# Two-layer hybrid decoder trunk: the first layer's loads in one written order, scale vectors turned on TensorE, bias table behind the projections

## The chip, the core and the metric

One core of a Trainium2 chip runs the whole program. Its engines work side by side, each through its own instruction stream in a fixed order: TensorE (PE) for products and transposes, VectorE (DVE), ScalarE (ACT), GpSimd (POOL), and SyncE (SP), which here issues the DMAs. An instruction that waits holds up all that stand behind it on its engine. The metric is device time in microseconds: the profiled execution took 2197.31 us, and the three timed runs 2196.4 to 2206.05 us.

## The reference

Two layers over 1024 tokens of width 1024, all in fp32. Each layer normalises, makes one projection of 1312 columns and gives its parts to three mixers; their outputs are concatenated, projected and added; then comes a SwiGLU feed-forward part.

```python
for l in range(DEPTH):
    h = rms_norm(x, attn_norm[l])
    proj = h @ w_in[l]                                   # 1024 x 1312
    q_a, k_a, v_a, u_b, cq_c, ckv_c, kr_c = jnp.split(proj, split_idx, axis=-1)
    out_a = swa_mixer(q_a, k_a, v_a, swa_q_gain[l], swa_k_gain[l], swa_sinks[l], rel_bias)
    out_b = pool_mixer(u_b, pool_w[l], pool_scale[l])
    out_c = mla_mixer(cq_c, ckv_c, kr_c, positions, ...)
    x = x + jnp.concatenate([out_a, out_b, out_c], axis=-1) @ w_out[l]
    h = rms_norm(x, ffn_norm[l])
    x = x + (jax.nn.silu(h @ w_gate[l]) * (h @ w_up[l])) @ w_down[l]
```

The sliding-window mixer (`swa_mixer`) adds a relative-position bias of 128 x 256 per head, made from a 32-row table; the latent-attention mixer (`mla_mixer`) turns parts of its queries and keys by the cosine and sine of position times frequency. Gains are vectors that scale columns.

## The kernel before, in words

The kernel is written with a planner: the program gives instructions and their dependences, the planner runs a simulation of the engines and writes each engine's order. Two means bend that order: a block of high priority, and `issue_after(i)`, which puts instructions behind `i` on their engine's queue without waiting for more than that. Tiles come from pools; a pool with `bufs=n` has n buffers for a name, and a load into one waits until the readers of its old content are done.

Each layer has `phase1` (projection, sliding-window and pooling mixers), `phase2` (latent attention and output projection) and `phase34` (feed-forward). All products of fp32 values are made of three passes, high part with high, high with low, low with high; so every weight is split into two tiles: ACT scales and rounds it to the high part (L351), DVE subtracts to get the low part (L352).

`phase1` works on eight tiles of 128 tokens, t = 0 to 7. `head(t)` (L330) squares the rows of x for the norm and turns the tile on PE in eight transposes, splitting it into `hT`. The weights of `w_in` (1024 x 1312) come in three column blocks of 512, 400 and 400, each in eight row blocks of 128 (L345 to L352): a load by SP into `raw` (five buffers), scaled by the norm's gain `gn`, a vector loaded element by element with rows on partitions (L316). `wa` holds the first block, `wb` the other two. For each tile `proj(0, 512)` (24 products, L381 to L383) gives q and k, which become `qk` (L390), are normalised, turned by transposes `tq` and scaled by `gq` into `qs`; `proj(512, 512)` and `proj(1024, 288)` give the rest. The accumulators `acc` have two banks, so the first group of tile 1 comes behind the last of tile 0. Then come the transposes of the pooling and latent parts, the scores `s` of the sliding window, the bias added (L523), the exponentials (L528), transposes `tp` of the weights and the product with `vt` (L543, L544).

`tables` (L133), called once in layer 0 behind the weight loop, builds what all tiles need. The bias: a small product of `rel` and `hot` (L146), copied into `flip` (L148), written to DRAM as `rows` (L150), read back with overlapping rows into `T`, which borrows the key tile `kr5` (L153), reversed by a product with `flip` (L159), copied to `bias` (L160) and kept in DRAM for layer 1 (L161). The gains: `gq`, `gk`, `pscale`, `gc`, `gm`, `gmk` are loaded element by element into columns (L175 to L204). The angles: some 45 short DVE instructions on tiles `rr` that borrow five `raw` buffers, and two sines on ACT (L207 to L280). The remaining tiles of x (L172) are loaded here too, in a chain of `issue_after`. The weights of layer 0 stand in a high-priority block, `tables` does not.

`phase2` loads `mla_w_kvb` and `mla_w_qb` (L589, L596) and scales their splits by `gc`; `early_out` (L806) loads parts of `w_out` into `raw3`, splits them into `wo0` to `wo4`, and multiplies with `mh`, adding rows `xt` of the input. `gn2`, the gain of the feed-forward norm spread to all partitions, is loaded at L875; the planner may issue that as soon as its buffer is free. The pools of `phase2` are laid over those of `phase1` in memory, so its first loads and writes wait for particular tiles of `phase1`.

Of the kernel before, what the change touches and what calls it, by code (L numbers as in the profile page):

```python
# [36 lines left out]
def trunk(ctx: ExitStack, tc: tile.TileContext, A, out):  # L37
# [55 lines left out]

    with tc.high_priority():
        sy.dma_start(xrow[0], A["x"][0, 0:P, :])
        sy.dma_start(ident, A["ident"])
# [6 lines left out]
    for l in range(DEPTH):  # L103
        xsrc = A["x"][0] if l == 0 else xres
        G = dict(
            ident=ident, xm=xm, xrow=xrow, krr=krr, rc=rc, cosT=cosT, sinT=sinT, sinks=sinks,
            pscale=pscale, invc=invc, nhalf=nhalf, gq=gq, gm=gm, cmask=cmask, identr=identr, rn=rn, gc=gc, g32=g32, xsrc=xsrc, dram=dram, gap=gap, xp=xp, gns=ExitStack(), bias_keep=bias_keep)
        phase1(nc, tc, A, l, pool, split, f, bcast, G, (gq, gk, gmk, dram) if l == 0 else None)
# [24 lines left out]
def tables(nc, tc, load, A, bcast, early, one, evq, ps, kr5, G, more):  # L133
    ve, sc, gp, te, sy = nc.vector, nc.scalar, nc.gpsimd, nc.tensor, nc.sync
    gq, gk, gmk, dram = more
    gm, sinks, bias, cosT, sinT = G["gm"], G["sinks"], G["bias"], G["cosT"], G["sinT"]

    rel = one.tile([P, 6], F32, name="rel")
    gp.memset(rel, NEG)
    sy.dma_start(rel[0:32], A["rel_bias"])  # L140
    hot = evq.tile([P, 512], F32, name="hot", tag="qk")[:, 0:384]
    sy.dma_start(hot[0:33], A["hot"])
    flip = evq.tile([P, 5, 128], F32, name="flip", tag="dup")
    sy.dma_start(flip[:, 0], A["flip"])
    acc = ps.tile([P, 512], F32, name="po")
    te.matmul(acc[0:6, 0:384], rel[0:33], hot[0:33], start=True, stop=True)  # L146
    vec = flip[0:6, 1:4]
    sc.copy(vec, acc[0:6, 0:384].rearrange("p (a b) -> p a b", a=3))  # L148
    rows = dram.tile([6, 384], F32, name="rows")
    sy.dma_start(rows.rearrange("h (a b) -> h a b", a=3), vec)  # L150
    base = rows[0:6, 0:256]
    T = kr5.bitcast(F32).rearrange("p a b c -> p (a b c)")
    sy.dma_start(T.rearrange("p (h j) -> p h j", h=6),  # L153
                 bass.AP(base.tensor, base.offset, [[1, P], [384, 6], [1, 256]]))
    b2 = bias.rearrange("p h j -> p (h j)")
    for i in range(3):
        acc = ps.tile([P, 512], F32, name="po")
        c = slice(512 * i, 512 * i + 512)
        te.matmul(acc, flip[:, 0], T[:, c], start=True, stop=True)  # L159
        sc.copy(b2[:, c], acc)  # L160
    sy.dma_start(G["bias_keep"], bias)  # L161

    pin = [load]

    def after(*calls):
        with tc.issue_after(pin[0].ins):
            for call in calls:
                last = call()
        pin[0] = last

    def xload(t):
        return sy.dma_start(G["xrow"][t], A["x"][0, t * P : (t + 1) * P, :])  # L172

    for h in range(2):
        after(lambda: sy.dma_start(gq[64 * h : 64 * h + 64], A["swa_q_gain"].rearrange("l d -> d l")),  # L175
              lambda: sy.dma_start(gk[64 * h : 64 * h + 64], A["swa_k_gain"].rearrange("l d -> d l")))
    ve.scalar_tensor_tensor(out=gq, in0=gq, scalar=0.125, in1=gk, op0=ALU.mult, op1=ALU.mult)
    after(lambda: xload(2))
    after(lambda: sy.dma_start(
        sinks, A["swa_sinks"].rearrange("l h -> (l h)").unsqueeze(0).to_broadcast([P, 12])  # L180
        .rearrange("p (l h) -> p l h", l=DEPTH)))
    after(lambda: sy.dma_start(G["invc"], A["invc"]))
    after(lambda: sy.dma_start(G["pscale"], A["pool_scale"].rearrange("l (k p) -> p l k", p=P)))
    slots = [early.tile([P, 4, NT, 16], F32, name="rr", tag="raw", bufs=5) for _ in range(5)]
    free = [t[:, i] for t in slots for i in range(4)]
    ps0 = free.pop().rearrange("p a b -> p (a b)")
    pos, posf, ifr = ps0[:, 0:8].bitcast(I32), ps0[:, 8:16], ps0[:, 16:32]
    after(lambda: sy.dma_start(pos, A["positions"][0].rearrange("(t p) -> p t", p=P)))
    ve.tensor_copy(posf, pos)
    after(lambda: sy.dma_start(ifr, bcast(A["invf"], 16)))  # L190
    for t in range(3, NT):
        after(lambda: xload(t))
    for l in range(DEPTH):
        after(lambda: sy.dma_start(G["gc"][:, l, 0:2], A["mla_q_a_gain"][l].rearrange("(k p) -> p k", p=P)))
        after(lambda: sy.dma_start(G["gc"][:, l, 2:3], A["mla_kv_a_gain"][l].rearrange("(k p) -> p k", p=P)))
        after(lambda: sy.dma_start(G["g32"][l], bcast(A["mla_q_rope_gain"][l], 32)))
    mask = one.tile([P, P], F32, name="mask", tag="ub")
    after(lambda: sy.dma_start(mask, A["cmask"]))
    sc.copy(G["cmask"], mask)
    sc.copy(G["identr"], G["ident"])  # L200
    gp.memset(gm, 1.0)
    gp.memset(gmk, 1.0)
    after(lambda: sy.dma_start(gm[0:64], A["mla_q_nope_gain"].rearrange("l d -> d l")))
    after(lambda: sy.dma_start(gmk[0:64], A["mla_k_nope_gain"].rearrange("l d -> d l")))  # L204
    ve.scalar_tensor_tensor(out=gm, in0=gm, scalar=float(96.0 ** -0.5), in1=gmk, op0=ALU.mult, op1=ALU.mult)
# [77 lines left out]
def phase1(nc, tc, A, l, pool, split, f, bcast, G, setup):  # L283
# [3 lines left out]
    with ExitStack() as ph:  # L287
# [26 lines left out]
        gn = early.tile([P, KT], F32, name="gn")  # L314
        with tc.high_priority() if l == 0 else nullcontext():
            sy.dma_start(gn, A["attn_norm"][l].rearrange("(k p) -> p k", p=P))  # L316
# [11 lines left out]
        behind = []  # L328

        def head(t):  # L330
# [3 lines left out]
            rows[t] = rstd_of(nc, ms, 1, G["nhalf"])  # L334
            hT = hTs[t] = hp[t % 2].tile([P, 2, KT, P], F32R, name="hT")
            for h in range(2):
# [3 lines left out]
                split(hT[:, 0, 4 * h : 4 * h + 4], hT[:, 1, 4 * h : 4 * h + 4], tp)  # L340

        with tc.high_priority() if l == 0 else nullcontext():
            if l == 0:
                head(0)
            for i, (c0, n) in enumerate(((0, 512), (512, 400), (912, 400))):  # L345
                for k in range(KT):
                    raw = early.tile([P, 512], F32, name="raw", bufs=5)[:, 0:n]
                    load = sy.dma_start(raw, A["w_in"][l, k * P : (k + 1) * P, c0 : c0 + n])
# [957 lines left out]
```

## Time and profile before

| | us |
|---|---|
| median of three runs | 2201.54 |
| lowest and highest run | 2196.4, 2206.05 |
| profiled execution | 2197.31 |
| its span, first to last instruction | 2195.5 |
| PE busy in it | 2104.7 |
| DVE, ACT, POOL busy | 1697.9, 1089.6, 974.3 |

In the profile's rows a timeline line gives the start in us, the duration in us, the engine, the source line, the operation, the tile written and those read, partitions by elements, and in brackets how long the engine had been idle and what it had waited for. SPq is the DMA issuer: its duration is that of the issue, not of the transfer. In a table by stretches each engine's busy time is followed by its count of instructions, then come the clock granted to PE (1.00 is full), the mean share of the DMA engines and GB/s.

### The profile page before, as it was taken

To read this page: it belongs to the slowest core of one execution; us is meant where nothing else is said; L and a number is where in the kernel's file an instruction comes from. 1 tells how busy PE (TensorE), PEld (TensorE's weight loads), DVE (VectorE), ACT (ScalarE), POOL (GpSimd) and SP (SyncE) were. 2 spreads that over 40 slices of the span, in tenths; PEclk is the share of its full clock that TensorE was granted. 3 is DMA by queue.
4 is the path that set the end of the run, shared out by engine and by line. 5 is a ranking of instruction groups with operands and counts; after the bars stand their busy time and mean duration, and the time that the engine had idled before them with its cause. 6 is when DMAs were issued, how large, how long until landed. Compare 5 with 4: busy or idle time off the path is not lost.

```text
span 2195.5 us, 29665 instructions
## 1 busy us (share of the span) xinstructions
PE 2104.7 (96%) x10420; PEld 1757.7 (80%) x10420; DVE 1697.9 (77%) x2595; ACT 1089.6 (50%) x2300; POOL 974.3 (44%) x916
## 2 busy tenths in 40 slices
PE   6998999999999999999989989999999999999999
PEld 4887788877888888788868867888778888887887
DVE  5567889889988888765765678887998888877657
ACT  5778667564344434321257786776634343343111
POOL 1433656336545443532613445462564544425215
PEclk8999999999999999999999999999999999999999
DMA  7002211234443434985540022113244443459754
GB/s 221 1 1 77 77 68 49 96 98 146 152 162 135 163 134 151 411 344 187 186 157 1 1 90 87 63 49 121 81 144 169 148 163 135 152 218 412 271 201 163
DMA packets 137933, 312.16 MB, mean 142 GB/s; under 512 B 17298, under 2 KB 68153, under 8 KB 137785
## 3 DMA queue, kind: packets, MB, share of 16 engines
q1 hardware_dynamic: 137784, 310.27, 39.7%
q8 instruction: 83, 1.36, 0.3%
q14 instruction: 66, 0.53, 0.1%
HBM read 203.53 MB, written 106.70 MB: 141 GB/s over the span
## 4 chain that ended last, share of the span: by engine, by line
PE 71%; DVE 11%; DMA 8%; ACT 5%; issue 2%; POOL 2%; SPq 1%; DVEq 0%; ACTq 0%; POOLq 0%
PE gu L1156 10%; PE gu L1154 10%; PE gu L1155 10%; PE dn L1001 5%; PE dn L1003 5%; PE dn L1002 5%; PE acc L381 3%; PE acc L382 3%; PE acc L383 3%; DMA rw<-in_w_down_dram 2%; PE tp L763 2%; PE po L804 1%; PE po L802 1%; DMA ga<-gd 1%; PE po L803 1%
## 5 line engine op out<-in xcount | busy, mean ns | idle before, releaser
L1156 PE MATMUL gu<-T,sb 128*128 128x512 f32 x704 | 275.2, 391 | 8.8 <-DVE sb L58 8.7
L1154 PE MATMUL gu<-T,sb 128*128 128x512 f32 x704 | 275.0, 391 | 3.9 <-DVE B L58 1.6
L1155 PE MATMUL gu<-T,sb 128*128 128x512 f32 x704 | 274.2, 390 | 0.0
L1001 PE MATMUL dn<-op,ga 128*128 128x512 f32 x616 | 240.1, 390 | 8.1 <-DMA ga<-gd 8.1
L1002 PE MATMUL dn<-op,ga 128*128 128x512 f32 x616 | 240.4, 390 | 0.0
L58 ACT CAST go<-xm 128x512 fp32r<-128x512 f32 x154 | 94.9, 620 | 292.3 <-POOL xm L1188 103.0
L1003 PE MATMUL dn<-op,ga 128*128 128x512 f32 x616 | 239.7, 390 | 0.0
L950 POOL TENSOR_TENSOR rw<-rw 128x1536 f32<-128x1536 f32 (+1 forms) x32 | 112.0, 3511 | 253.7 <-DVE op L960 160.6
L1131 POOL TENSOR_TENSOR xm<-raw 128x512 f32<-128x512 f32 x44 | 67.2, 1529 | 325.8 <-DMA raw<-in_w_up_dram 136.6
L959 ACT CAST op<-rw 128x1536 fp32r<-128x1536 f32 (+1 forms) x56 | 76.8, 1376 | 261.6 <-PE dn L1003 250.6
L58 DVE TENSOR_TENSOR go<-xm,go 128x512 fp32r<-128x512 f32 x154 | 157.5, 1033 | 41.1 <-ACT go L58 37.0
L58 ACT CAST sb<-raw 128x512 fp32r<-128x512 f32 x180 | 110.3, 616 | 115.3 <-PE gu L1156 92.2
L1156 PEld LDWEIGHTS gu<-T,sb 128*128 128x128 f32 x704 | 132.2, 188 | 40.1 <-DVE sb L58 12.9
L1154 PEld LDWEIGHTS gu<-T,sb 128*128 128x128 f32 x704 | 132.2, 188 | 33.7 <-ACT sb L58 3.5
L1188 POOL TENSOR_TENSOR xm<-xm 128x512 f32<-128x512 f32 x88 | 142.8, 1631 | 28.6 <-DVE go L58 18.4
L58 DVE TENSOR_TENSOR sb<-raw,sb 128x512 fp32r<-128x512 f32 x180 | 154.0, 856 | 0.9
L1155 PEld LDWEIGHTS gu<-T,sb 128*128 128x128 f32 x704 | 132.3, 188 | 27.7
L960 DVE TENSOR_TENSOR op<-rw,op 128x1536 fp32r<-128x1536 f32 (+1 forms) x56 | 113.8, 2032 | 40.7 <-ACT op L959 39.7
L1001 PEld LDWEIGHTS dn<-op,ga 128*128 128x128 f32 x616 | 116.0, 188 | 33.7 <-issue 8.6
L1154 PE MATMUL gu<-B,A 128*128 128x512 f32 x336 | 132.5, 395 | 3.9 <-ACT B L58 3.9
L1003 PEld LDWEIGHTS dn<-op,ga 128*128 128x128 f32 x616 | 116.0, 188 | 24.3
L1002 PEld LDWEIGHTS dn<-op,ga 128*128 128x128 f32 x616 | 115.9, 188 | 24.0
(324 smaller groups left out, 6084.3 us busy)
## 6 DMA issues: line engine op xcount, KB each, us to landing
gd<-go SPq DMA_DIRECT2D x154, 512.0 KB, 2.9
ga<-gd SPq DMA_DIRECT2D x154, 512.0 KB, 5.8
raw<-in_w_gate_dram SPq DMA_DIRECT2D x22, 1024.0 KB, 5.7
raw<-in_w_up_dram SPq DMA_DIRECT2D x22, 1024.0 KB, 6.6
rw<-in_w_down_dram SPq DMA_DIRECT2D x44, 512.0 KB, 8.0
xp<-xt SPq DMA_DIRECT2D x32, 256.0 KB, 2.0
old<-xp SPq DMA_DIRECT2D x16, 512.0 KB, 4.3
xp<-xm SPq DMA_DIRECT2D x16, 512.0 KB, 2.9
```

The costliest lines, as they stand in the source:

```text
L58: return sc.copy(hi, src), ve.tensor_tensor(out=lo, in0=src, in1=f(hi), op=ALU.subtract)
L950: gp.tensor_tensor(out=o, in0=a, in1=b, op=ALU.subtract)
L959: sc.copy(t[:, 0], q[b])
L960: ve.tensor_tensor(out=t[:, 1], in0=q[b], in1=f(t[:, 0]), op=ALU.subtract)
L1001: te.matmul(acc, S_[:, j, 0, ts], T_[:, 0, j], start=j == 0, stop=False)
L1002: te.matmul(acc, S_[:, j, 0, ts], T_[:, 1, j], start=False, stop=False)
L1003: te.matmul(acc, S_[:, j, 1, ts], T_[:, 0, j], start=False, stop=j == h - 1)
L1131: gp.tensor_tensor(out=s1, in0=q["A21"], in1=q["A22"], op=ALU.add)
L1154: te.matmul(acc, s[:, 0, k], b[:, 0, k], start=k == 0, stop=False)
L1155: te.matmul(acc, s[:, 0, k], b[:, 1, k], start=False, stop=False)
L1156: te.matmul(acc, s[:, 1, k], b[:, 0, k], start=False, stop=k == HK - 1)
L1188: gp.tensor_tensor(out=q[o], in0=q[a], in1=q[b], op=op)
```

## The change

Layer 0's start is rewritten as a class `Boot`; `tables` is dissolved into it.

- One order for the DMAs of the start: `load` puts each behind the one before on SP. Only four go by ACT's queue: the identity, the attention norm's gain of both layers, and the two gains of the sliding window.
- `raw` has eleven buffers in layer 0 instead of five; hot rows, the read-back table, angles and mask use them too.
- Vectors are loaded as rows (`gv`) and turned on PE (`turn`): `gna` (both layers' norm gains, at the start), `gqk` (behind tile 0's first group), `gains` (14 columns, behind tile 0's projections). Layer 1 copies its `gn` from `gna` on POOL.
- `head(0)` squares its rows only after its first split. Tile 1 is loaded and made ready between the first column block and the others; its first projection group (`group0(1)`) goes ahead of tile 0's second.
- A small load stands behind each weight of the second and third blocks (`steps`); the table is read back after the last weight (`fourth`), in three pieces; the bias products come behind tile 0's projections and pooling part (`bias`).
- In all tiles of both layers `proj(512, 512)` is queued behind the last product named in `G["mm"]`; `gn2` is queued behind the load of `mla_w_qb`.

```diff
+class Boot:
+    def load(self, dst, src):
+        if self.pin is None:
+            self.pin = self.nc.sync.dma_start(dst, src)
+        else:
+            with self.tc.issue_after(self.pin.ins):
+                self.pin = self.nc.sync.dma_start(dst, src)
+        return self.pin
+    def raw(self):
+        return self.early.tile([P, 512], F32, name="raw", bufs=11)
+    def turn(self, dst, rows, n):
+        te, sc = self.nc.tensor, self.nc.scalar
+        acc = self.psg.tile([P, 4, P], F32, name="ta")
+        te.transpose(acc[:, 0, 0:n], rows[0:n], self.G["ident"][0:n, 0:n])
+        sc.copy(dst, acc[:, 0, 0:n])
+    def first(self):
...
+        self.xload(0)
+        sc.dma_start(G["ident"], A["ident"])
+        sc.dma_start(gv[0:16, 0], A["attn_norm"].rearrange("l (k p) -> (l k) p", p=P))
+        for r, n in ((0, "swa_q_gain"), (2, "swa_k_gain")):
+            sc.dma_start(gv[r : r + 2, 2].rearrange("l (a d) -> l a d", a=2), A[n].unsqueeze(1).to_broadcast([2, 2, 64]))
+        self.nc.gpsimd.memset(gv[:, 1], 1.0)
+        self.turn(G["gna"], gv[:, 0], 16)
...
+    def steps(self):
...
+        self.load(rel[0:32], A["rel_bias"])
+        yield
+        hot = self.raw()[:, 0:384]
+        self.load(hot[0:33], A["hot"])
...
+        te.matmul(acc[0:6, 0:384], rel[0:33], hot[0:33], start=True, stop=True)
+        sc.copy(flip[0:6, 1:4], acc[0:6, 0:384].rearrange("p (a b) -> p a b", a=3))
+        yield
+        self.load(flip[:, 0], A["flip"])
+        yield
...
+        self.load(rows.rearrange("h (a b) -> h a b", a=3), self.flip[0:6, 1:4])
+        self.base = rows[0:6, 0:256]
+        yield
+        self.xload(2)
+        yield
+        self.load(G["invc"], A["invc"])
+    def fourth(self):
...
+        for i in range(3):
+            T = self.raw()
+            self.load(T.rearrange("p (h j) -> p h j", h=2),
+                      bass.AP(base.tensor, base.offset + 768 * i, [[1, P], [384, 2], [1, 256]]))
+            self.T.append(T)
+        self.rope()
+        mask = self.raw()[:, 0:P]
+        self.load(mask, A["cmask"])
...
+    def bias(self):
...
+        self.turn(g, self.gv[:, 1], 14)
...
+        for i in range(3):
+            acc = self.ps.tile([P, 512], F32, name="po")
+            te.matmul(acc, self.flip[:, 0], self.T[i], start=True, stop=True)
+            sc.copy(b2[:, 512 * i : 512 * i + 512], acc)
...
         with tc.high_priority() if l == 0 else nullcontext():
             if l == 0:
+                boot.first()
+                small = boot.steps()
                 head(0)
             for i, (c0, n) in enumerate(((0, 512), (512, 400), (912, 400))):
                 for k in range(KT):
-                    raw = early.tile([P, 512], F32, name="raw", bufs=5)[:, 0:n]
-                    load = sy.dma_start(raw, A["w_in"][l, k * P : (k + 1) * P, c0 : c0 + n])
+                    raw = early.tile([P, 512], F32, name="raw", bufs=5 if l else 11)[:, 0:n]
+                    dma(raw, A["w_in"][l, k * P : (k + 1) * P, c0 : c0 + n])
...
-                if l == 0 and i == 1:
-                    sy.dma_start(xrow[1], A["x"][0, P : 2 * P, :])
+                    if l == 0 and i:
+                        next(small, None)
+                if l == 0 and i == 0:
+                    boot.xload(1)
+                    head(1)
+            if l == 0:
+                for _ in small:
+                    pass
+                boot.fourth()
+        dma(gkr, bcast(A["mla_k_rope_gain"][l], 32))
...
+        if l == 0:
+            for t in range(3, NT):
+                boot.xload(t)
...
+            qk, r8 = ahead.pop(t, None) or group0(t)
+            if l == 0 and t == 0:
+                with tc.issue_after(G["mm"].ins):
+                    boot.second()
...
-            acc = proj(512, 512)
+            if l == 0 and t == 0:
+                ahead[1] = group0(1)
+            with tc.issue_after(G["mm"].ins):
+                acc = proj(512, 512)
...
+            if l == 0 and t == 0:
+                boot.bias()
+                with tc.issue_after(boot.pin.ins):
+                    sy.dma_start(G["bias_keep"], G["bias"])
...
-                sy.dma_start(gn2, bcast(A["ffn_norm"][l], D))
+                with tc.issue_after(kvload.ins):
+                    sy.dma_start(gn2, bcast(A["ffn_norm"][l], D))
```

`rope` loads positions and frequencies through `load` and calls the angle code, which is unchanged and now a function `angles`; all of `fourth` stands in the high-priority block.

More of the change, by code (lines that the diff above doesn't have):

```diff
@@ L107, in trunk @@
             pscale=pscale, invc=invc, nhalf=nhalf, gq=gq, gm=gm, cmask=cmask, identr=identr, rn=rn, gc=gc, g32=g32, xsrc=xsrc, dram=dram, gap=gap, xp=xp, gns=ExitStack(), bias_keep=bias_keep)
[L108 removed]
+        G["gna"], G["gains"], G["gqk"] = gna, gains, gqk
+        phase1(nc, tc, A, l, pool, split, f, bcast, G)
         phase2(nc, tc, A, l, pool, split, f, bcast, G)
@@ L130, in rope @@
     eng.tensor_tensor(out=dst, in0=a, in1=b, op=ALU.add)
[L133 to L205, printed above, removed]
@@ new lines, with __init__, xload, second @@
+class Boot:
+    def __init__(self, nc, tc, A, bcast, early, ps, psg, G):
+        self.nc, self.tc, self.A, self.bcast, self.early, self.ps, self.psg, self.G = nc, tc, A, bcast, early, ps, psg, G
+        self.pin = None
+    def load(self, dst, src):
[5 more added lines that the diff above has]
+        return self.pin
+    def xload(self, t):
+        self.load(self.G["xrow"][t], self.A["x"][0, t * P : (t + 1) * P, :])
+    def raw(self):
[6 more added lines that the diff above has]
+    def first(self):
+        A, G, sc = self.A, self.G, self.nc.scalar
+        gv = self.gv = self.early.tile([P, 3, P], F32, name="gv")
+        self.xload(0)
[5 more added lines that the diff above has]
+        self.turn(G["gna"], gv[:, 0], 16)
+    def second(self):
+        g = self.G["gqk"]
+        self.turn(g, self.gv[:, 2], 4)
+        self.nc.vector.scalar_tensor_tensor(out=self.G["gq"], in0=g[:, 0:2], scalar=0.125, in1=g[:, 2:4],
+                                            op0=ALU.mult, op1=ALU.mult)
+    def steps(self):
+        A, G, gv = self.A, self.G, self.gv[:, 1]
+        sc, gp, te = self.nc.scalar, self.nc.gpsimd, self.nc.tensor
+        rel = self.early.tile([P, 6], F32, name="rel")
+        gp.memset(rel, NEG)
+        self.load(rel[0:32], A["rel_bias"])
+        yield
+        hot = self.raw()[:, 0:384]
+        self.load(hot[0:33], A["hot"])
+        flip = self.flip = self.early.tile([P, 4, 128], F32, name="flip")
+        acc = self.ps.tile([P, 512], F32, name="po")
[4 more added lines that the diff above has]
+        yield
+        for r, n in ((0, "pool_scale"), (4, "mla_q_a_gain"), (8, "mla_kv_a_gain")):
+            self.load(gv[r : r + (2 if r == 8 else 4)], A[n].rearrange("l (k p) -> (l k) p", p=P))
+            yield
+        for r, n in ((10, "mla_q_nope_gain"), (12, "mla_k_nope_gain")):
+            self.load(gv[r : r + 2, 0:64], A[n])
+            yield
+        self.load(G["sinks"], A["swa_sinks"].rearrange("l h -> (l h)").unsqueeze(0).to_broadcast([P, 12])
+                  .rearrange("p (l h) -> p l h", l=DEPTH))
+        yield
+        rows = G["dram"].tile([6, 384], F32, name="rows")
+        self.load(rows.rearrange("h (a b) -> h a b", a=3), self.flip[0:6, 1:4])
+        self.base = rows[0:6, 0:256]
+        yield
+        self.xload(2)
+        yield
+        self.load(G["invc"], A["invc"])
+    def fourth(self):
+        A, G, sc, base = self.A, self.G, self.nc.scalar, self.base
+        self.T = []
+        for i in range(3):
[6 more added lines that the diff above has]
+        self.load(mask, A["cmask"])
+        sc.copy(G["cmask"], mask)
+        sc.copy(G["identr"], G["ident"])
+        for l in range(DEPTH):
+            self.load(G["g32"][l], self.bcast(A["mla_q_rope_gain"][l], 32))
+    def bias(self):
+        te, sc, G, g = self.nc.tensor, self.nc.scalar, self.G, self.G["gains"]
+        self.turn(g, self.gv[:, 1], 14)
+        self.nc.vector.scalar_tensor_tensor(out=G["gm"], in0=g[:, 10:12], scalar=float(96.0 ** -0.5), in1=g[:, 12:14],
+                                            op0=ALU.mult, op1=ALU.mult)
+        b2 = G["bias"].rearrange("p h j -> p (h j)")
+        for i in range(3):
+            acc = self.ps.tile([P, 512], F32, name="po")
+            te.matmul(acc, self.flip[:, 0], self.T[i], start=True, stop=True)
+            sc.copy(b2[:, 512 * i : 512 * i + 512], acc)
+    def rope(self):
+        A, G, ve, sc, bcast = self.A, self.G, self.nc.vector, self.nc.scalar, self.bcast
+        slots = [self.raw().rearrange("p (i a b) -> p i a b", i=4, b=16) for _ in range(5)]
+        free = [t[:, i] for t in slots for i in range(4)]
+        ps0 = free.pop().rearrange("p a b -> p (a b)")
+        pos, posf, ifr = ps0[:, 0:8].bitcast(I32), ps0[:, 8:16], ps0[:, 16:32]
+        self.load(pos, A["positions"][0].rearrange("(t p) -> p t", p=P))
+        self.load(ifr, bcast(A["invf"], 16))
+        ve.tensor_copy(posf, pos)
+        angles(ve, sc, free, posf, ifr, G["cosT"], G["sinT"])
@@ L207, in tables, with angles @@
+def angles(ve, sc, free, posf, ifr, cosT, sinT):
     shp = [P, NT, 16]
```

68 lines of the change are left out of this document (37 added, 31 removed).

## The prediction

> **What bounds the kernel now.** First the page: which engine is full, and where it is not.
>
> ```profile
> PE 2104.7 (96%) x10420; PEld 1757.7 (80%) x10420; DVE 1697.9 (77%) x2595; ACT 1089.6 (50%) x2300; POOL 974.3 (44%) x916
> PE   6998999999999999999989989999999999999999
> ```
>
> TensorE (PE) is busy 2104.7 of 2195.5 us, so 90.8 us of the whole span are idle, and the thinnest slices (6 and 9, 9 tenths in slices of 55 us) are the first. The change is aimed there. Next the busy time by stretches of the first 250 us:
>
> ```profile
> core 0: us, PE busy (x) PEld busy (x) DVE busy (x) ACT busy (x) POOL busy (x), PEclk, DMA share, GB/s
> 0.00:5.44 5.44, 0.00 (x0) 0.00 (x1) 0.00 (x0) 2.08 (x2) 0.79 (x12) 1.00 0.66 171
> 5.44:14.00 8.56, 7.39 (x24) 5.05 (x25) 4.81 (x8) 5.50 (x11) 0.80 (x2) 1.00 0.93 302
> 14.00:30.00 16.00, 8.17 (x24) 3.34 (x22) 8.23 (x15) 10.32 (x20) 2.72 (x4) 0.73 0.67 204
> 30.00:44.70 14.70, 12.28 (x61) 9.46 (x60) 7.58 (x16) 8.66 (x17) 1.04 (x4) 0.94 0.72 195
> 44.70:67.40 22.70, 20.88 (x106) 17.18 (x107) 14.72 (x64) 15.52 (x44) 5.51 (x15) 0.92 0.31 109
> 67.40:187.00 119.60, 118.57 (x690) 103.52 (x691) 71.74 (x145) 90.04 (x249) 48.14 (x115) 1.00 0.02 6
> 187.00:250.00 63.00, 54.77 (x274) 44.25 (x272) 48.17 (x95) 44.93 (x118) 25.76 (x45) 0.92 0.29 95
> ```
>
> From 67.4 to 187 us PE is busy 118.57 of 119.60 us: whatever comes earlier at 67 should come earlier at 187. Before 67.4 there are three deficits: no product before 5.44, half a stage idle from 14 to 30, and DMA that falls from 302 to 204 GB/s although weights are missing. Now the milestones, from the timelines of ScalarE (ACT), of PE and of the DMA issuer SP. The line of `qk` (L390) stands right behind the first projection group of a token tile, so it is the clock of the tiles.
>
> ```profile
> 6.45 0.72 ACT L351 ACTIVATE wa<-raw,gn 128x512 fp32r<-128x512 f32 x1 [0.47 <-DMA raw<-in_w_in_dram]
> 16.44 0.72 ACT L351 ACTIVATE wa<-raw,gn 128x512 fp32r<-128x512 f32 x1
> 19.95 0.67 ACT L390 ACTIVATE qk<-acc,ms 128x512 f32<-128x512 f32 x1
> 36.41 0.63 ACT L351 ACTIVATE wb<-raw,gn 128x400 fp32r<-128x400 f32 x1 [0.85 <-DMA raw<-in_w_in_dram]
> 52.40 0.69 ACT L390 ACTIVATE qk<-acc,ms 128x512 f32<-128x512 f32 x1 [7.03 <-PE acc L383]
> 73.55 0.69 ACT L390 ACTIVATE qk<-acc,ms 128x512 f32<-128x512 f32 x1 [0.18 <-PE acc L383]
> ...
> 1.17 0.42 SPq L316 DMA_DIRECT2D gn<-in_attn_norm_dram  x1
> 1.64 0.57 SPq L96 DMA_DIRECT2D ident<-in_ident_dram  x1
> 17.37 0.42 SPq L875 DMA_DIRECT2D gn<-in_ffn_norm_dram  x1
> 18.43 15.12 SPq L348 DMA_DIRECT2D raw<-in_w_in_dram  x12
> ...
> 17.96 7.59 DMA kr<-rows
> ...
> 25.60 2.08 PE L159 MATMUL po<-kr,flip 128*128 128x512 f32 x2 [4.37 <-DMA kr<-rows]
> 31.26 1.27 PE L159 MATMUL po<-kr,flip 128*128 128x512 f32 x2
> 40.93 0.29 PE L383 MATMUL acc<-wb,hT 128*128 128x288 f32 x1
> 44.67 0.50 PE L381 MATMUL acc<-wa,hT 128*128 128x512 f32 x1 [0.80 <-ACT cn L439]
> ```
>
> Call g0(t) the first group (24 products) of tile t and B(t) its other 48. Tile 0 goes: weights of g0 split by 17.2, `qk` at 19.95; last weight of B split at 37.0, B(0) done at 41.2; only then g0(1), which ends at 52.4; tile 2's g0 ends at 73.55. The last twelve weight loads take SP from 18.43 to 33.55, because two other things are in the stream at that moment: `ffn_norm` (128 x 1024 fp32, 0.52 MB, not wanted for hundreds of us) and the bias table read back (128 x 6 x 256 fp32, 0.79 MB, 7.59 us), and because SP waits for weight buffers:
>
> ```profile
> SPq L348 <- DVE wb L352: 5.1, 5, 1.7
> SPq L348 <- DMA raw<-in_w_in_dram: 4.8, 3, 3.9
> ```
>
> PE also stands 4.37 us in its written order before the bias products, which nothing needs until tile 0's attention.
>
> **The change, part by part.**
>
> *Start.* `gn` and `ident` leave SP (0.42 + 0.57 us of issue) for ACT's queue, behind whose four issues the first ACT work waits for x anyway. The first weight goes out 1.0 us earlier: first split 6.45 - 1.0 = 5.4. The turned `gn` costs one small transpose and one small copy, hidden in the wait for that weight.
>
> *Weights of g0.* 8 loads of 128 x 512 fp32, 0.262 MB each. With eleven buffers nothing waits for a buffer, so DMA paces them; at 302 GB/s that is 0.87 us each, longer than ACT's 0.72. Last split starts at 5.4 + 7 x 0.87 = 11.5 instead of 16.44. `qk` follows 3.5 us behind it today (19.95 - 16.44); I take 2.8, since PE is less far behind: qk(0) at 14.3.
>
> *x of tile 1, g0(1) ahead.* 0.52 MB more is 1.7 us: landed at about 13.1. Eight transposes and two split pairs make it 16; g0(1) is 24 products. Their spacing:
>
> ```profile
> 46.36 0.63 PE L383 MATMUL acc<-wa,hT 128*128 128x512 f32 x1
> 46.79 0.63 PE L381 MATMUL acc<-wa,hT 128*128 128x512 f32 x1
> ...
> 49.34 0.39 PE L382 MATMUL acc<-wa,hT 128*128 128x512 f32 x1
> 49.57 0.40 PE L383 MATMUL acc<-wa,hT 128*128 128x512 f32 x1
> ...
> 36.94 0.29 PE L381 MATMUL acc<-wb,hT 128*128 128x288 f32 x1
> 37.07 0.39 PE L382 MATMUL acc<-wb,hT 128*128 128x512 f32 x1
> ```
>
> 0.23 us each at full rate, 0.43 after a pause, 0.13 for the 288-wide ones. So g0(1) lasts 5.5 us and ends at 21.5. Today the half rate lasted from 44.67 to about 48.7, behind 3.5 us that held only transposes, some 2 us lost. The Trainium skill's page "TensorE: Matmul & The Clock Gate", section "Part 1: The HAM clock gate", says that the array falls to half rate after an idle window of about 3.4 us and needs as long a busy one to return; the trace agrees here. By that rule g0(1), put between g0(0) and B(0), also keeps the rate up, and the sum would be the same, unless a weight is over 3.4 us late, which would cost those 2 us again.
>
> *Weights of B.* 16 x 0.205 MB, x of tile 2 (0.52 MB) and about 0.15 MB of small loads: 3.95 MB behind 13.1. At 302 GB/s they land by 26.2, at the 204 GB/s of today's stretch by 32.5. The second half of B's products needs the third column block, which starts to land at about 19; B(0) is 24 x (0.23 + 0.13) = 8.6 us and can begin at 21.5: end 30.1. At the slow rate its end is 32.5 + 2 = 34.5. I take 30.1, since the stream is what the written order and the eleven buffers give back to DMA. Each small load takes an SP slot of about 0.45 us; one weight and one small load per 0.87 us keep up with 302 GB/s, so these are covered.
>
> So g0(0), g0(1) and B(0) are done at 30.1 instead of 52.4: 22.3 us.
>
> *What is owed afterwards.* From 52.40 to 73.55, 21.15 us, PE did the rest up to g0(2) at a full pace. The new order owes the same, plus the bias products (three pairs, 1.27 us each warm, 2.08 cold: 3.8 to 6.2, take 3.8) and about 1.5 us of transposes and scores that stood ahead of 52.4 today: 26.5, so qk(2) at 56.6 without new stalls, a gain of 17.0.
>
> *New stalls.* The bias table is read back behind the last weight: issue at about 26, 7.59 us by today's row, so landed by 33.6. PE has B(1) (8.6 us) to do meanwhile; but it runs in its written order, and today it stood 4.37 us at this very wait. 0 to 7.6; I take 1.5. Behind the table on SP come positions, frequencies, mask, `g32`, `gkr`, `pool_w` and x of tiles 3 to 7; tile 3 is wanted only some 40 us on. The angle chain:
>
> ```profile
> 40.00:66.00 26.00, 8.76 (x45) 0.62 (x2) 0.93 0.40 124
> ```
>
> That is VectorE's 8.76 us in 45 instructions on tile `rr`. They are now in the high-priority block, so they may go as one piece ahead of tile 0's softmax and the splits of hT(2). Covered by B(1) and the bias products (12.4 us) unless these splits stand behind it: 0 to 8.8; I take 2.0. Together 3.5: gain at tile 2 13.5.
>
> *The swa gains* are now rows turned on TensorE instead of columns loaded element by element; today `gq` is late and holds tile 0's queries:
>
> ```profile
> 40.59 0.16 DVE L177 SCALAR_TENSOR_TENSOR gq<-gq,gk 128x2 f32<-128x2 f32 x1 [2.88 <-DMA gk<-in_swa_k_gain_dram]
> ```
>
> It lies inside the 22.3 us; nothing is added for it.
>
> *Handover to phase 2 at 187.* Eleven buffers instead of five, and `gv` and `flip`, push the projection weights up by about 16 KB per partition, so phase 2's tiles wait for other ones. PE idles 63.0 - 54.77 = 8.2 us there. The staging tiles `raw3`, `wo0` to `wo2` now lie over the g0 weights, free earlier; `xt` and `mh` over the B weights, free later. Between -4 (half the idle time) and +4; I take 0.
>
> *Layer 1.* `ffn_norm` no longer stands in the weight stream, `gn` is a copy on POOL instead of a load:
>
> ```profile
> 1121.34 0.40 SPq L875 DMA_DIRECT2D gn<-in_ffn_norm_dram  x1
> ...
> PE acc L381 <- ACT wb L351: 1.2, 1, 1.2
> ```
>
> At most 0.52 MB / 302 GB/s = 1.7 us; I take 1.0, near the 1.2 that PE waits for those splits. Queueing B behind the last g0 product costs nothing where both are ready, as in the 118.57 of 119.60.
>
> **Sum.** 13.5 + 1.0 = 14.5 us. The profiled execution took 2197.3 us (2195.5 span and 1.8 around it); it becomes 2182.8. The median of the runs is 2201.54, 4.2 above it: 2187.0. All else that the planner reorders I leave at zero, plus or minus 4.
>
> **Rivals.**
>
> 1. *The stream does not run at 302, or the waits move.* B(0) at 34.5 takes 4.4 away; a wait for the table of 4.4 as today instead of 1.5 takes 2.9: gain 7.2, 2194. For it: 302 GB/s was held for only 8.56 us, and PE's written order has met this wait before. Against: the two large strangers and the buffer waits are gone. The Trainium skill's page "DMA: Bandwidth & Descriptors", section "Bandwidth", gives 138 GB/s for 64 KB and 341 for 1 MB and advises transfers of at least 1 MiB; our loads lie between, and 302 with several in flight agrees with neither end.
>
> 2. *Slower: PE stands behind the table.* If its products and tile 0's scores are placed straight behind B(0), PE waits out the whole chain: the read 7.6, products and copies in series at the cold rate, 3 x (2.08 + 0.58) - 3.8 = 4.2, the angles 8.8, four table loads on ACT of 1.28 for the two sines, 5.1, and two cold restarts, 4.0: 29.7 us against the 17.0 won, less 1.0 in layer 1: 2213. Rows for the copy and the table load:
>
> ```profile
> 27.71 0.58 ACT L160 COPY bias<-po 128x512 f32<-128x512 f32 x1 [1.01 <-PE po L159]
> 58.96 1.28 ACT L277 ACT_TABLE_LOAD   x1
> ```
>
>    It decides from 29 us of stalls. For it: the 4.37. Against: B(1) and g0(2), 14 us of products, do not depend on it.
>
> 3. *The handover gains too*: stalls of 1 instead of 3.5 and 4 us less idle time at 187: 2180.5.
>
> 4. *No effect*: ACT and not DMA paces the splits. 8 x 0.72 + 16 x 0.63 = 15.8 us of 25; only with ACT's other work of the stretch does it come near. It would look like rival 1.
>
> **Chances.** Forecast (2182 to 2190) 0.48; rival 1 with 4 0.32; rival 2 0.11; rival 3 0.09. The measurement tells about 0.5%, 11 us, from no change: faster means below 2190.5. Forecast and rival 3, less a little at the border: 0.56; same 0.33; slower 0.11. The range runs from rival 3 with 2 us more, 2178, to 2208: rival 1's slow stream with both stalls at their bounds (7.6 + 8.8) and 4 us lost at the handover, a gain of 17.0 - 4.4 - 16.4 - 4 + 1 = -6.8.
>
> **What would show it.** Right: `qk` of tile 0 at about 14, of tile 1 near 22, of tile 2 near 60; the last `wb` split near 27; DMA near 300 GB/s up to 26 us; no PE wait over 3 us on the table; 19 to 21 us per tile from there on; PE's idle time from tile 7 on within 4 us of today's. Wrong: `qk` of tile 2 beyond 66 (stream or table), an hT split behind the angles, or idle time that comes back behind tile 7 or in layer 1.

## The result and the profile after

The changed kernel takes 2219.4 us (median of nine runs, 2214.57 to 2226.61), the kernel before 2201.54 beside it (nine runs, 2194.27 to 2208.63). The ratio is 1.0078, 95% interval 1.0062 to 1.0093: 17.9 us slower, where 14.5 us less were forecast. The profiled execution took 2220.96 us.

The start came out as planned. Milestones of the changed kernel, from ACT's timeline (L455 is `qk`, L406 the weight splits); the rows are tiles 0, 1, 2 and 7, and the last weight splits:

```profile
18.72 0.66 ACT L455 ACTIVATE qk<-acc,ms 128x512 f32<-128x512 f32 x1
27.81 0.69 ACT L455 ACTIVATE qk<-acc,ms 128x512 f32<-128x512 f32 x1
54.73 0.67 ACT L455 ACTIVATE qk<-acc,ms 128x512 f32<-128x512 f32 x1
158.32 0.69 ACT L455 ACTIVATE qk<-acc,ms 128x512 f32<-128x512 f32 x1
...
25.06 2.70 ACT L406 ACTIVATE wb<-raw,gna 128x400 fp32r<-128x400 f32 x5
```

Tile 2 was at 73.55, so 18.8 us are won there; tile 7 was at 175.24, so 16.9 are left at the end of phase 1. The stretches of the changed kernel, columns as before:

```profile
0.00:5.44 5.44, 0.70 (x4) 0.70 (x4) 0.00 (x0) 1.58 (x2) 0.87 (x11) 1.00 0.66 222
5.44:14.00 8.56, 7.10 (x26) 5.30 (x26) 6.71 (x10) 8.04 (x14) 0.80 (x2) 1.00 0.99 337
14.00:30.00 16.00, 15.98 (x70) 11.05 (x69) 12.42 (x25) 14.51 (x30) 4.02 (x7) 1.00 0.84 248
30.00:44.70 14.70, 14.70 (x82) 12.23 (x81) 13.66 (x57) 7.77 (x22) 3.83 (x7) 1.00 0.60 221
```

PE was busy 8.17 of 16.00 us from 14 to 30; now it is 15.98, and it stays full to 44.7. Yet the whole is longer, and PE is not more idle but busier. The page's line of busy times and its costliest groups, the changed kernel first:

```profile
PE 2142.4 (97%) x10423; PEld 1766.2 (80%) x10423; DVE 1690.1 (76%) x2595; ACT 1088.0 (49%) x2301; POOL 979.7 (44%) x916
...
L1234 PE MATMUL gu<-T,sb 128*128 128x512 f32 x704 | 277.9, 395 | 6.4 <-DVE sb L58 6.3
L1232 PE MATMUL gu<-T,sb 128*128 128x512 f32 x704 | 278.9, 396 | 3.1 <-ACT sb L58 1.5
...
L1079 PE MATMUL dn<-op,ga 128*128 128x512 f32 x616 | 243.7, 397 | 4.8 <-DMA ga<-gd 4.8
```

```profile
L1156 PE MATMUL gu<-T,sb 128*128 128x512 f32 x704 | 275.2, 391 | 8.8 <-DVE sb L58 8.7
L1154 PE MATMUL gu<-T,sb 128*128 128x512 f32 x704 | 275.0, 391 | 3.9 <-DVE B L58 1.6
...
L1001 PE MATMUL dn<-op,ga 128*128 128x512 f32 x616 | 240.1, 390 | 8.1 <-DMA ga<-gd 8.1
```

PE's sum rose from 2104.7 to 2142.4 us with three instructions more. The feed-forward products (`gu` for gate and up, `dn` for down) are the same in number, their code is untouched, and one takes 395 to 397 ns where it took 390 or 391. Their ends overlap the next ones, so start to start is the better measure. PE's timeline inside the down products, the first and the last of seven in a row, the changed kernel and then the kernel before:

```profile
999.65 0.40 PE L1079 MATMUL dn<-op,ga 128*128 128x512 f32 x1
...
1001.05 0.40 PE L1079 MATMUL dn<-op,ga 128*128 128x512 f32 x1
```

```profile
999.83 0.39 PE L1002 MATMUL dn<-op,ga 128*128 128x512 f32 x1
...
1001.19 0.39 PE L1002 MATMUL dn<-op,ga 128*128 128x512 f32 x1
```

Six steps take 1.40 us in the one and 1.36 in the other: 233.3 against 226.7 ns. It is not the clock. The stretch from 700 to 900 us, the changed kernel and the kernel before, columns as above:

```profile
700.00:900.00 200.00, 200.00 (x863) 161.86 (x862) 159.95 (x190) 78.25 (x132) 88.49 (x54) 1.00 0.49 181
```

```profile
700.00:900.00 200.00, 200.00 (x883) 165.30 (x882) 166.23 (x195) 77.19 (x132) 90.84 (x56) 1.00 0.48 173
```

PE is busy all 200 us at a granted clock of 1.00 in both, with 863 instructions after and 883 before.

What differs there is where the operands lie. Of the two operands of a product the stationary one is loaded as weights (the profile's PEld, one load for each product) and the other is the moving one. The built program's tiles stand on two stacks in each partition. The left one holds the constants, x and the stationary operands: `sb`, made of gate and up weights, and `ga`, the gated rows. The right one holds moving operands: `T1`, `T4` and the `B` tiles, made of turned rows of x, and `op`, made of down weights. The change took four small constants out (`pscale`, `gk`, `gmk`, `gc`: four slots of 32 bytes) and put three in (`gna` 64, `gqk` 32, `gains` 64 bytes). So the left stack, `sb` and `ga` with it, stands 32 bytes higher; the right one stays. In the kernel before, `sb` (byte 110048 of the partition) and `T1` (208864) differ by a multiple of 512 bytes, as do `ga` (38368) and `op` (192480). In the changed kernel they are 32 bytes off. `T2` and `T3` lie on the left stack themselves; of every seven groups of gate/up products these two still come down to 226 or 227 ns after their first few products, and the others stay at 231 to 235.

### The profile page after: what moved, and what is told of

Same layout as the page of the kernel before. It is cut to its first block, busy times and chain, and to the rows that moved or that the text cites. A ratio compares the mean times of both kernels' runs of the same rounds, so it can differ in the third digit from the quotient of the medians.

```text
span 2219.2 us, 29675 instructions
## 1 busy us (share of the span) xinstructions
PE 2142.4 (97%) x10423; PEld 1766.2 (80%) x10423; DVE 1690.1 (76%) x2595; ACT 1088.0 (49%) x2301; POOL 979.7 (44%) x916
## 3 DMA queue, kind: packets, MB, share of 16 engines
q8 instruction: 83, 1.36, 0.2%
## 4 chain that ended last, share of the span: by engine, by line
PE 77%; DVE 9%; DMA 5%; ACT 4%; POOL 3%; issue 2%; SPq 0%; DVEq 0%; POOLq 0%; ACTq 0%
PE gu L1232 11%; PE gu L1234 11%; PE gu L1233 11%; PE dn L1079 6%; PE dn L1080 6%; PE dn L1081 6%; PE acc L445 3%; PE acc L447 3%; PE acc L446 3%; PE tp L840 2%; DMA rw<-in_w_down_dram 2%; PE po L881 1%; PE po L880 1%; PE po L879 1%; PE ss L816 1%
## 5 line engine op out<-in xcount | busy, mean ns | idle before, releaser
L1234 PE MATMUL gu<-T,sb 128*128 128x512 f32 x704 | 277.9, 395 | 6.4 <-DVE sb L58 6.3
L1232 PE MATMUL gu<-T,sb 128*128 128x512 f32 x704 | 278.9, 396 | 3.1 <-ACT sb L58 1.5
L1233 PE MATMUL gu<-T,sb 128*128 128x512 f32 x704 | 278.2, 395 | 0.0
L1079 PE MATMUL dn<-op,ga 128*128 128x512 f32 x616 | 243.7, 397 | 4.8 <-DMA ga<-gd 4.8
L1080 PE MATMUL dn<-op,ga 128*128 128x512 f32 x616 | 244.2, 396 | 0.0
L1081 PE MATMUL dn<-op,ga 128*128 128x512 f32 x616 | 243.4, 396 | 0.0
L58 DVE TENSOR_TENSOR go<-xm,go 128x512 fp32r<-128x512 f32 x154 | 152.9, 1002 | 40.8 <-ACT go L58 37.0
```

Source lines behind the costliest of these rows:

```text
L58: return sc.copy(hi, src), ve.tensor_tensor(out=lo, in0=src, in1=f(hi), op=ALU.subtract)
L1079: te.matmul(acc, S_[:, j, 0, ts], T_[:, 0, j], start=j == 0, stop=False)
L1080: te.matmul(acc, S_[:, j, 0, ts], T_[:, 1, j], start=False, stop=False)
L1081: te.matmul(acc, S_[:, j, 1, ts], T_[:, 0, j], start=False, stop=j == h - 1)
L1232: te.matmul(acc, s[:, 0, k], b[:, 0, k], start=k == 0, stop=False)
L1233: te.matmul(acc, s[:, 0, k], b[:, 1, k], start=False, stop=False)
```

## The experiments

**First set: is it the address?** The constant `nhalf` (-0.5 in 32 columns, of which at most 18 are read) sits low on the left stack. Widening it by 8 columns moves the stack by 32 bytes and changes no other instruction's place in any engine's order.

`e1_before_left32`, the kernel before:

```diff
-    nhalf = cst.tile([P, 32], F32, name="nhalf")
+    nhalf = cst.tile([P, 40], F32, name="nhalf")
```

> The kernel before, with one constant tile 32 bytes per partition larger; nothing else changes, so every tile of the left stack moves by 32 bytes and those of the right stack stay. Address theory: in the feed-forward part the stationary operand then lies on a multiple of 64 bytes and the moving operand of five products in seven, and of all of the last product, 32 bytes off it; their start-to-start rises from 227 to 232 to 235 ns, some 4490 products by 6.7 ns: 30 us slower, about 2232. Rival (the loss of the changed kernel comes from waits or the order of its work): within 4 us of before.

`e2_after_left32`, the same edit in the changed kernel:

> The changed kernel with the same 32 bytes more, so that its left stack lies as in the kernel before (32 bytes off a multiple of 64, like the right stack). Address theory: 227 ns per product again in the feed-forward part, about 30 us less than the changed kernel, 2189, and 13 to 19 us faster than before. Rival: 2219 as the changed kernel.

`e3_after_right32`, the changed kernel with the right stack moved (`gap` is the kernel's own helper that leaves bytes free on a stack):

```diff
-    xres = dram.tile([S, D], F32, name="xres")
+    gap(ctx, "shim", 32, "right"); xres = dram.tile([S, D], F32, name="xres")
```

> The changed kernel with 32 bytes taken from the right stack instead, so that both stacks lie on multiples of 64. If what counts is that stationary and moving operand lie alike, 227 ns and about 2189; if the left stack's own place on a multiple of 64 were what costs, 232 to 235 ns and 2219.

`e4_after_left64`, the changed kernel with `nhalf` of 48 columns:

> The changed kernel with 64 bytes more: left stack still on a multiple of 64, right stack 32 off. Address theory (modulo 64): as the changed kernel, 2219, products at 232 to 235 ns. If any shift helped, or the place modulo 128 counted, it would be faster.

Measured against 2199.73 us of the kernel before (seven runs, 2197.16 to 2204.35): e1 2222.66, ratio 1.0102 (1.0078 to 1.0126); e2 2221.33, 1.0093 (1.0076 to 1.0109); e3 2217.59, 1.0075 (1.0058 to 1.0091); e4 2224.0, 1.0107 (1.0090 to 1.0125). e1 settles the first question: 32 bytes alone make the kernel before 22.9 us slower (30 were expected), and its down products read as those of the changed kernel do:

```profile
L1001 PE MATMUL dn<-op,ga 128*128 128x512 f32 x616 | 244.0, 397 | 4.5 <-DMA ga<-gd 4.5
```

e2 and e3 missed. They were to bring the speed back, on the theory that the two operands need only agree modulo 64; they left it at 233.3 ns. So the period, if there is one, is longer.

**Second set: what period, and does the changed kernel win once this is put right?**

`e5_after_as_before`, the changed kernel; the left stack is then where the kernel before had it:

```diff
-    nhalf = cst.tile([P, 32], F32, name="nhalf")
+    nhalf = cst.tile([P, 24], F32, name="nhalf")
```

> The changed kernel with nhalf 24 columns wide instead of 32, so that the constants take 32 bytes less per partition and every tile of the left stack has the address that it had in the kernel before; the order of the instructions on every engine is that of the changed kernel. If the address of the stationary operand against the moving one is what cost the time: back-to-back 512-wide products at 226 to 227 ns in gate/up and down, 23 to 30 us less than the changed kernel, 2190 to 2196 us, 5 to 11 us under the kernel before. If the changed order of the program costs the time elsewhere: within 4 us of 2219.

`e6_before_left128` and `e7_before_left256`, the kernel before with `nhalf` of 64 and of 96 columns:

> The kernel before with nhalf 64 columns wide, the left stack 128 bytes higher. If the two operands must agree modulo 128 or less: 227 ns and 2200 us as before. If modulo 256 or more: 232 to 234 ns in down and in five of seven gate/up products, about 2222 us.

> The kernel before with nhalf 96 columns wide, the left stack 256 bytes higher. If the operands must agree modulo 256: 227 ns and 2200 us. If modulo 512: 232 to 234 ns, about 2222 us.

`e8_after_right480`, the changed kernel with `gap(ctx, "shim", 480, "right")` in the place shown for e3:

> The changed kernel with the right stack 480 bytes lower, the left stack as in the changed kernel, so that left and right agree modulo 512 again (both 0; in the kernel before both were 480). The planner orders some work otherwise. If agreement is what counts and not the address itself: 226 to 227 ns and within 6 us of the changed kernel with nhalf of 24 columns (2190 to 2200). If the address itself counts: 232 to 234 ns and about 2219.

All of it together; "off" is how far the left operand stands above a multiple of 512 bytes from the right one, and the spacings are means of start to start over some 3600 gate/up and 1800 down products of each trace:

| run | off, bytes | gate/up, ns | down, ns | median, us |
|---|---|---|---|---|
| before | 0 | 226.9 | 226.7 | 2201.5 |
| after | 32 | 232.0 | 233.3 | 2219.4 |
| e1 (before) | 32 | 232.0 | 233.3 | 2222.7 |
| e2 (after) | 64 | 231.9 | 233.3 | 2221.3 |
| e3 (after) | 64 | 231.9 | 233.3 | 2217.6 |
| e4 (after) | 96 | 232.6 | 234.3 | 2224.0 |
| e6 (before) | 128 | 231.6 | 232.5 | 2222.7 |
| e7 (before) | 256 | 226.9 | 226.8 | 2201.7 |
| e5 (after) | 0 | 226.9 | 226.7 | 2197.1 |
| e8 (after) | 0 | 226.9 | 226.8 | 2197.7 |

A shift of 256 bytes costs nothing and one of 128 costs all: of the distances tried here, 0 and 256 bytes are fast and 32, 64, 96 and 128 slow, as if the stationary and the moving operand had to lie a multiple of 256 bytes apart. The place itself does not count: in e8 the left stack stands 32 bytes above, the right one 480 bytes below where e5 has it. e5 against the kernel before, 2201.51 in that set: 0.9985 (0.9971 to 1.0000). e8: 0.9979 (0.9965 to 0.9994). e5 fell just short of what was expected: 22.3 us below the changed kernel instead of 23 to 30, and 4.4 below the kernel before instead of 5 to 11.

The page of e5 shows how the price comes about:

```profile
PE 2105.5 (96%) x10423; PEld 1756.4 (80%) x10423; DVE 1693.2 (77%) x2595; ACT 1086.5 (50%) x2301; POOL 982.0 (45%) x916
...
L1234 PE MATMUL gu<-T,sb 128*128 128x512 f32 x704 | 275.5, 392 | 9.5 <-DVE sb L58 9.4
L1232 PE MATMUL gu<-T,sb 128*128 128x512 f32 x704 | 275.4, 391 | 5.0 <-DVE B L58 2.0
...
L1079 PE MATMUL dn<-op,ga 128*128 128x512 f32 x616 | 239.8, 391 | 9.3 <-DMA ga<-gd 9.3
```

3696 gate/up products at 5.1 ns and 1848 down products at 6.6 make 31.0 us. But slower products wait less for their operands: the idle times of these three groups are 14.3 us in the changed kernel and 23.8 in e5, 9.5 more. That leaves 21.5; the medians, 2219.4 and 2197.1, differ by 22.3.

**Third set: where is the rest?** e5 is 4.4 us faster than the kernel before, not 14.5, although its start is as early as the changed kernel's. Lead over the kernel before, read off the timelines: 16.4 us at `qk` of tile 7 (158.8 against 175.2), 16.4 at the first gate/up product (442.6, 459.0), 13.4 at the last down product of layer 0 (1092.7, 1106.1), but 0.5 at the first gate/up product of layer 1 (1542.9, 1543.4). It goes in layer 1's mixers, whose code the change touches in few places. One is the pin: in both layers `proj(512, 512)`, the start of a tile's second group, is queued behind the last product named before it. The waits of PE in layer 1, from 1085 to 1560 us of e5, and the one line about `hT` of the kernel before:

```profile
PE acc L445 <- ACT hT L58: 6.2, 6, 1.4
PE th L389 <- DVE xm L1069: 3.2, 1, 3.2
PE po L620 <- DVE xm L624: 3.2, 1, 3.2
```

```profile
PE acc L381 <- ACT hT L58: 0.7, 1, 0.7
```

How such a wait arises, in e5's timeline of PE:

```profile
1135.69 0.30 PE L447 MATMUL acc<-wb,hT 128*128 128x288 f32 x1
1135.83 0.60 PE L389 MATMUL th<-ident,xm 128*128 128x128 f32 x4
...
1137.00 0.27 PE L598 MATMUL s<-kr,qs 128*128 128x128 f32 x1
1138.63 0.50 PE L445 MATMUL acc<-wa,hT 128*128 128x512 f32 x1 [1.36 <-ACT hT L58]
```

The transposes of a tile stand next to its products with only a few scores between, and PE waits until ACT and DVE have split them. A tile's first group needs `hT` in two halves of twelve products each. In the kernel before the planner lays products of the same tile's second group, which need no more of `hT`, between the two halves and further on. The pin forbids just that. Counted at 24 products a group, the third tile goes twelve on `wa`, ten on `wb`, then the rest, from which these rows are (L382 on `wb` inside a run on `wa`):

```profile
1158.97 0.39 PE L382 MATMUL acc<-wa,hT 128*128 128x512 f32 x1
1159.20 0.39 PE L382 MATMUL acc<-wb,hT 128*128 128x512 f32 x1
1159.43 0.39 PE L383 MATMUL acc<-wa,hT 128*128 128x512 f32 x1
```

`e9_no_pin_layer1` is e5 and this (`nullcontext()` does nothing):

```diff
-            with tc.issue_after(G["mm"].ins):
+            with tc.issue_after(G["mm"].ins) if l == 0 else nullcontext():
                 acc = proj(512, 512)
```

> The changed kernel with nhalf of 24 columns, and with the pin that holds a tile's second projection behind the last product of its first one kept in layer 1 out: it then acts in layer 0 alone. From the last down product of layer 0 to the first gate/up product of layer 1 the kernel before takes 437 to 442 us and the changed kernel with 24 columns 450 us. If that pin, which the diff sets in both layers, makes the difference: 437 to 443 us again, and 2185 to 2191 us for the whole. If something else in layer 1 does (the gain copied by POOL, the later transposes of tile 1): 447 to 451 us and 2194 to 2199.

`e10_wa_aligned` is e9 with one tile more on the left stack:

```diff
-        wt = pool(ph, f"p1t_{l}")
+        gap(ph, f"p1m_{l}", 128); wt = pool(ph, f"p1t_{l}")
```

> As e9, with 128 bytes left free ahead of the wa buffers, so that the 16 wa tiles of the first projection stand at a multiple of 256 bytes from hT, where they stood 128 off. If agreement modulo 256 is all that counts, back-to-back products of wa come at 226 to 227 ns in place of 232.4, 384 of them, 2 us off the whole beside e9. If phase 1 is slow for another reason: 231 to 233 ns still, and within 2 us of e9.

`e11_before_pin` is the kernel before with `G["mm"]` set at the last product of `proj`, and:

```diff
-            acc = proj(512, 512)
+            with tc.issue_after(G["mm"].ins) if l else nullcontext(): acc = proj(512, 512)
```

> The kernel before with that pin alone added, in layer 1 alone. If the pin is what layer 1 lost: 446 to 451 us from the last down product of layer 0 to the first gate/up product of layer 1, and 2208 to 2213 us. If not: 437 to 443 us and 2198 to 2204.

`e12_no_g0_ahead` is e9 without the early first group:

```diff
-            if l == 0 and t == 0:
+            if 0:
                 ahead[1] = group0(1)
```

> As e9, without the first projection of tile 1 ahead of the second of tile 0. If that step fills time in which TensorE would wait for the late weight slices: the first projection's 24 products come later at full speed (24 x 0.232 = 5.6 us), qk of tile 2 comes 3 to 6 us later than in e9, and the whole is 3 to 6 us longer. If the weights come in time anyway: within 2 us of e9.

Measured against 2201.79 us of the kernel before (23 runs, 2194.89 to 2207.7):

| run | median, us | ratio to before | interval |
|---|---|---|---|
| e9 | 2187.75 | 0.9938 | 0.9923 to 0.9952 |
| e10 | 2187.22 | 0.9932 | 0.9911 to 0.9953 |
| e11 | 2208.98 | 1.0027 | 1.0012 to 1.0043 |
| e12 | 2201.91 | 1.0001 | 0.9986 to 1.0015 |

*e9 and e11.* Without the pin in layer 1 the changed program gains 9.3 us (2197.08 to 2187.75); with it alone the kernel before loses 7.2 (2.6 to 9.5 by the interval). The stretch from the last down product of layer 0 to the first gate/up product of layer 1, for the kernel before, e7 (the same program but for `nhalf`), e5, e9 and e11:

```profile
1106.13:1543.44 437.31, 409.78 (x2412) 353.47 (x2411) 324.18 (x670) 303.65 (x766) 185.67 (x277) 0.98 0.22 71
```

```profile
1110.08:1552.19 442.11, 415.15 (x2413) 358.56 (x2411) 324.12 (x670) 303.75 (x766) 185.27 (x277) 0.97 0.21 69
```

```profile
1092.74:1542.94 450.20, 418.13 (x2412) 357.12 (x2411) 324.19 (x668) 301.30 (x764) 187.42 (x277) 0.97 0.20 67
```

```profile
1092.21:1533.88 441.67, 415.71 (x2413) 356.65 (x2411) 322.47 (x668) 301.85 (x764) 183.89 (x277) 0.97 0.20 68
```

```profile
1110.30:1556.25 445.95, 415.66 (x2413) 359.43 (x2411) 324.08 (x670) 302.66 (x766) 181.02 (x277) 0.96 0.21 68
```

Two executions of one order of instructions differ by 4.8 us here (437.31 and 442.11), so a pair of traces does not settle 8. All traces together do: the same stretch takes 446.8 to 450.2 us in the six with the pin in the changed order (after, e2, e3, e4, e5, e8) and 437.3 to 442.1 in the seven without it (before, e1, e6, e7, e9, e10, e12), and the medians agree. e5 has 32.1 us of idle PE in the stretch, e9 26.0, and of the 6.2 us of waits for `hT` 0.7 are left. e11's 445.95 lies just under the 446 that was expected, and its 2208.98 within the 2208 to 2213. But its waits for `hT` are short, so the way in which the pin costs time there is not shown. The waits of PE for `hT` that ACT wrote, e9 and then e11:

```profile
PE acc L445 <- ACT hT L58: 0.7, 1, 0.7
```

```profile
PE acc L381 <- ACT hT L58: 1.6, 2, 0.9
```

*e10.* The spacing of the `wa` products fell from a mean of 232.6 to 229.0 ns, about half of them to 226 or 227, and the whole stayed where e9 was. So agreement modulo 256 helps in another loop too. The other half are in the main those that follow an interruption (a transpose, a wait, a product of another kind): of the first three spacings behind one, 22% are at 226 or 227 ns, from the eleventh on all are. The aligned gate/up products of the kernel before do the same, 233 ns in the first two and 226.7 from the eleventh on. Short runs therefore gain little, and the feed-forward part, with its long ones, gains most.

*e12.* The expectation of 3 to 6 us was too small: 14.2. The 14 to 30 us of e9 and of e12, and the two longest waits of PE there in e12:

```profile
14.00:30.00 16.00, 15.90 (x68) 10.99 (x69) 12.19 (x23) 14.37 (x29) 4.28 (x7) 1.00 0.86 257
```

```profile
14.00:30.00 16.00, 10.91 (x45) 7.93 (x46) 11.94 (x23) 13.12 (x26) 4.27 (x7) 0.79 0.84 253
...
PE th L389 <- DMA xm<-in_x_dram: 3.4, 2, 2.2
PE acc L445 <- ACT wb L406: 2.9, 1, 2.9
```

PE stands 5 us more, and the granted clock of the stretch is 0.79 instead of 1.00. `qk` of tile 2 comes at 66.6 instead of 55.5, 11 us later, where the first group alone is 5.6 us of products. The early group is worth twice its length, since it keeps the work and the clock up. The granted clock of e12 is 1.00 from 14.0 to 21.2 us and 0.50 from 21.3 to 28.0: it fell inside the first of the two waits. (The Trainium skill, "TensorE: Matmul & The Clock Gate", "Part 1: The HAM clock gate", has the rate fall after an idle window of about 3.4 us. The wait itself is 2.9 us long; with the transposes ahead of it, no product started from 17.69 to 21.76. Whether transposes count as idle no run here shows.)

## Why the prediction was wrong

*The start: right in kind, 5 us too cautious.* `qk` of tile 2 was put at 60 and came at 54.73: the two stalls (3.5 us) did not come, and the table is not among PE's waits of the first 80 us, all of which are these, in the changed kernel:

```profile
PE th L389 <- DMA ident<-in_ident_dram: 4.7, 1, 4.7
PE th L389 <- DVE hT L58: 1.2, 1, 1.2
PE ta L528 <- DVE kr L58: 0.7, 1, 0.7
PE th L389 <- DMA xm<-in_x_dram: 0.3, 1, 0.3
```

The steps ahead of it were off in a way that cancelled. The first weight split came at 6.59, not 5.4, since the turned gain `gna` was copied only at 6.38. `qk` of tiles 0 and 1 came at 18.72 and 27.81, not 14 and 22, because ACT's row of work paces the start (busy 14.51 of the 16.00 us, without a wait for a weight), as in rival 4, and not DMA. PE fills the time with transposes and products of both tiles: the second group of tile 0 starts at 23.70, behind the 48 products of both first groups, so little is lost by it. The last `wb` splits end at 27.8; 27 was forecast.

*The early group of tile 1: right in kind, too small.* It was to fill 5.5 us; e12 shows that without it the whole gain is gone.

*The handover at 187, put at zero: right.* e5 leads by 16.4 us at tile 7 and by 16.4 at the first gate/up product. Over all traces, `qk` of tile 7 comes at 158.8 us on average in the eight with the early group and at 174.5 in the five of the old order, 15.7 apart; the first gate/up product comes at 444.9 and 460.1, 15.2 apart. In the changed kernel's own execution the lead shrinks from 16.9 to 11.9 (447.1). Its clock was lower there; from 250 to 442 us, the changed kernel and then e5:

```profile
250.00:350.00 100.00, 96.16 (x584) 84.73 (x584) 89.65 (x220) 70.50 (x182) 58.00 (x59) 0.97 0.18 61
350.00:442.00 92.00, 89.14 (x553) 78.29 (x551) 71.49 (x121) 55.06 (x113) 32.02 (x25) 0.96 0.29 98
```

```profile
250.00:350.00 100.00, 95.95 (x601) 83.81 (x600) 90.79 (x223) 71.99 (x186) 59.43 (x59) 1.00 0.18 62
350.00:442.00 92.00, 87.95 (x561) 76.88 (x559) 73.84 (x125) 57.61 (x118) 31.67 (x27) 1.00 0.34 109
```

A clock 3 and 4% down over 192 us is an estimated 6.7 us, if the work scales with it: enough for the 5. It is scatter of single executions: e3 and e4, with the same order on PE, ACT and DVE, come to the first gate/up product at 442.4 and 443.9.

*Layer 1, put at 1.0 us gained: wrong.* "Queueing B behind the last g0 product costs nothing where both are ready" is the step. It was read off layer 0, where PE was full. In layer 1 `hT` is not ready, and what the planner had laid between its two halves was the cover for the split. The pin costs 9.3 us in the changed kernel (e5, e9), where waits for `hT` make 5.5 of the 8.5 us between the two traces; in the kernel before it costs 7.2 (e11), where waits for `hT` from ACT grow by only 0.9 us, and the cause of the rest stays open. Idle time that comes back in layer 1 stood among the prediction's own signs of being wrong. The 1.0 us that was to be gained there does not show either: without the pin the stretch takes 438.4 to 442.1 us in the changed order (e9, e10, e12) and 437.3 to 442.1 in the old one.

*"All else that the planner reorders I leave at zero, plus or minus 4": wrong by its silence.* The step that decided the sign is not in the sum at all. The prediction considers memory once, for what waits for what ("Eleven buffers instead of five, and `gv` and `flip`, push the projection weights up by about 16 KB"); that three constants for four move every later tile of the left stack by 32 bytes was costed at nothing. It cost 22.3 us, spread over most of 5544 products that the diff does not touch, and no bound of the range held it.

From e9 to the changed kernel the medians go 2187.75 + 9.3 for the pin + 22.3 for the 32 bytes = 2219.4; both terms are differences of these medians, so the sum is no check of its own. Without those two the change is worth 14.0 us in e9, and the forecast was 14.5. That they lie so close is partly luck: the start gave 15 to 16 us instead of 13.5, and layer 1 nothing instead of 1.0. The slower rival, PE standing behind the table, did not happen.

e9, the change with `nhalf` eight columns narrower and the pin in layer 0 alone, beats both kernels: 31.6 us below the changed one, 14.0 below the one before.

## What to carry to other kernels

When busy time of an engine grows with the same instructions, compare start to start and then the addresses: a constant added at the bottom of a stack moves everything above it, and in this kernel 32 bytes cost 1% of the time. In long runs of products like these, keep the stationary and the moving tile a multiple of 256 bytes apart, and look at it again after each change of memory, however small. And a pin that orders one stage well should be put in that stage only: elsewhere it takes away the planner's cover for the next wait.

## What was not expected of the hardware

Back-to-back 512-wide fp32 products take 226.7 ns when the two operands lie 0 or 256 bytes apart modulo 512 and a mean of 232 to 234 ns, in five of seven gate/up groups and in all down products, at 32, 64, 96 and 128 bytes, at the same granted clock of 1.00. No other distance was tried. After an interruption, aligned products take up to ten to settle at 226.7 ns (the kernel before, e10). The Trainium skill, "SBUF — State Buffer", under "A bandwidth-pool intuition that's wrong (but worth ruling out)", gives the load of the stationary operand a read port of its own, independent of the moving operand's. From that alone one would not expect what the traces show, a spacing that depends by 2 to 3% on the relative address of the two. By what mechanism, the runs do not show.
